# Modulation loads in the units of modulation products, and no such product in the latent stage

## The chip, the cores and the metric

The kernel runs on one core of one Trainium2 chip. The metric is the device time of one execution in microseconds (us). TensorE is PE in the profile (PEld its weight load), VectorE is DVE, ScalarE is ACT, GpSimd is POOL, SyncE is SP. Each engine works through its own instructions strictly in the order in which they were written.

## The reference

Two transformer layers and then a third, modulated one, for 256 tokens of width 2048, all in float32. Cut to what matters here:

```python
x = residual_update(x, mixer_a(rms_norm(x), w_in_a, w_out_a), ..., w_ple_proj[0], w_ple_gate[0])   # 16 stick-breaking heads
kv = shared_kv(x, ..., w_dkv, ..., w_uk, w_uv, cos, sin)                                      # latent k and v, rotary
x = residual_update(x, mixer_b(rms_norm(x), kv, w_in_b, ..., w_uq, w_out_b), ..., w_ple_proj[1], w_ple_gate[1])
# second_block, the modulated layer
mod = silu(c) @ w_ada + b_ada                 # one row of 2048 times 2048 x 12288
sh1, sc1, gt1, sh2, sc2, gt2 = split(mod, 6)
h = rms_norm_2(x) * (1 + sc1) + sh1           # then w_in, a convolution, a sparse attention, gates, w_o
x = x + gt1 * rms_norm_2(mixed)
h = rms_norm_2(x) * (1 + sc2) + sh2           # then a gated feed-forward
x = x + gt2 * rms_norm_2(f)
```

`mod` depends on `c` and `w_ada_2` alone. It can be worked out at any time before the third layer needs it.

## The kernel before

The program is written out by a planner, the class `Run`. The large products stand in a list of blocks, one per 512 columns of a weight matrix (`w_in_a`, `w_out_a`, ..., in the order of the reference). A block is cut into **units**: the six matmuls of 128x512 that multiply two chunks of 128 rows of a weight by one of the two token tiles (`t` = 0 or 1), each chunk as three products of a high and a low part (L421 to L423, or L344 in pairs of blocks), into a PSUM tile `acc` or `sc`. A unit takes some 1.36 us of PE. There are 1695 units, numbered by `self.u`; unit 66 begins at about 87 us of the trace, unit 260 at 397, unit 344 at 523, unit 408 at 616, unit 560 at 869, unit 1016 at 1561, unit 1112 at 1696. Units named below are those numbers.

Every two units need one item of weights: 512 KB loaded by SP into `wst` (4 buffers), then split by ACT into `wh` (L213) and by DVE into the rest `wl` (L214), about ten units ahead (`LEAD`), into 6 buffers each (`RING`). `pump()` writes these out.

After each unit `go`, `pair` or `flipped` calls `side()`. It first continues the small work that hangs behind the blocks (normalisation, attention heads, rotary turns, transposes with `tp` as their PSUM tile), and then the **modulation**. `mod` is worked out on DVE: 24 column chunks `q` of 512 columns by 16 row chunks `k`, 384 products. One product is a load of 256 KB of `w_ada_2` into a tile `ast` (3 buffers, `XBUF`; on POOL's queue, L329) and one DVE instruction that multiplies it by a column of silu(c) and adds it to `ada` (L568 for the first row chunk, L571 for the others). After the sixteenth, `ada_sum` adds `ada` over the partitions: ACT and DVE split it into `adh` (L584) and `adl` (L585), and five units later PE multiplies both by ones (L588, L589), for each half of the chunk.

The list `extra` holds the 384 products with the unit in which each is due. `spread` makes it: it takes the units of two stretches (for chunks 0 to 19 and for 20 to 23) that are `calm`, which leaves out the units around `turns` (12 units before to 19 after a block at which one layer's result is completed or the next one's weights are prepared ahead, or a `w_ple_proj` block) and those around `heads` (from 4 units before the first to 3 after the last of the blocks named there), and spreads the products evenly over the units that are left. `xc` counts products used, `xd` products loaded. A product is used in the first unit that is at or past its due unit; a load may be written up to 12 units ahead of the due unit if one of the three buffers is free. In the kernel before a unit does one of the two, which makes at most one product in two units.

The **latent stage** is `w_dkv` (units 408 to 432), the latent norm, `w_in_b` with POOL, ACT and DVE making the key rope `krr` (L1093) and the latent tiles `ckvh`, `ckvl` (L533, L535), and then `w_uk`, `w_uv`, `w_uq` with the 16 latent heads between them (units 496 to 560): for these heads POOL turns the ropes (L1086 to L1089) out of tiles `nat` that ACT copies from PSUM (L1141), DVE copies keys (`kT`, L1124) and divides (`wide`, L1252, L1254).

Of the kernel before, what the change touches and what calls it, by code (L numbers as in the profile page):

```python
# [29 lines left out]
XBUF = 3  # L30
# [105 lines left out]
class Run:  # L136
# [170 lines left out]
    def side(self):  # L307
        for rec in list(self.urgent):
            if not rec[2] and rec[1] <= self.u:
                self.advance(rec)  # L310
        for rec in self.slow:
            if rec[1] <= self.u:
                self.advance(rec)
        self.urgent, self.slow, self.active = ([r for r in x if not r[2]] for x in (self.urgent, self.slow, self.active))
        if (self.queue and len(self.active) < self.width and self.u >= self.last + self.space
                and all(r[2] for r in self.queue[0][3])):
            rec = self.queue.popleft()
            rec[1] = self.u
            self.active.append(rec)
            self.last = self.u  # L320
        self.step()
        if self.xc < self.xd and self.extra[self.xc][0] <= self.u:
            x = self.extra[self.xc]
            x[2](x[3])
            self.xc += 1
        elif (self.xd < len(self.extra) and self.xd - self.xc < XBUF and self.extra[self.xd][0] - 12 <= self.u):
            x = self.extra[self.xd]
            st = self.main.tile([P, NB], F32, tag="ast", bufs=XBUF, name="ast")
            self.nc.gpsimd.dma_start(st, x[1])  # L329
            x.append(st)  # L330
            self.xd += 1
# [111 lines left out]
def body(ctx, tc, a, out):  # L443
# [117 lines left out]
    def ada_chunk(q, k):  # L561
        c0 = q * NB

        def use(w):
            s = silu_c[:, k : k + 1]
            if k == 0:
                ada_acc[q] = main.tile([P, NB], F32, tag="ada", bufs=2, name="ada")
                nc.vector.tensor_scalar(ada_acc[q], w, s, None, op0=ALU.mult)  # L568
                return
            acc = ada_acc[q]  # L570
            nc.vector.scalar_tensor_tensor(acc, w, s, acc, op0=ALU.mult, op1=ALU.add)  # L571
            if k == 15:
                ada_done.setdefault(q // 4, []).append(run.later(ada_sum(q)))

        return a["w_ada_2"][0, k * P : (k + 1) * P, c0 : c0 + NB], use
# [60 lines left out]
    blocks = []  # L636
# [1226 lines left out]
    def spread(run):  # L1863

        uf = blocks[n_ffn].u0
        calm = lambda lo, hi: [u for u in range(lo, hi) if all(not b - 12 <= u < b + 20 for b in turns)
                               and not heads[0] - 4 <= u < heads[-1] + 4]
        heads = [b.u0 for b in blocks if b.w.tensor.name in (a["w_uk"].tensor.name, a["w_uq"].tensor.name)]
        turns = [b.u0 for b in blocks if b.enter is not None or b.ahead is not None or b.w.tensor.name == a["w_ple_proj"].tensor.name]
        xs = []  # L1870
        uc = conv_block.u0
        for qs, us in ((range(20), calm(100, uc - 30) + calm(uc + 290, uf - 110)), (range(20, 24), calm(uf + 40, uf + 300))):
            todo = [(q, k) for q in qs for k in range(16)]
            for i, (q, k) in enumerate(todo):
                xs.append([us[len(us) * i // len(todo)], *ada_chunk(q, k)])
        return xs

    run = Run(nc, main, psum, blocks, spread)
    run.go()
    ph.close()  # L1880
# [48 lines left out]
```

## Time and profile before

| | |
|---|---|
| median of 3 runs | 2538.36 us (2535.8 to 2538.81) |
| the profiled execution | 2536.7 us, its span 2534.9 us |
| granted TensorE clock, mean over the span | 0.994 |
| PE busy | 2471.3 us, 97% of the span |
| DVE busy | 1814.5 us, 72% |
| ACT busy | 1329.5 us, 52% |
| POOL busy | 283.6 us, 11% |
| moved by DMA | 562.51 MB, mean 222 GB/s |

The busy rows are sums over one execution; they say nothing of a single stage. Where an engine waits, the trace names the instruction that it waited with, the one that released it, the sum, how often and the longest. A DMA issue on POOL's queue counts as an instruction of POOL. The granted clock is the share of the full TensorE clock (2.4 GHz) that the chip gave: 1.00 is the upper level, 0.50 the lower.

### The profile page before, as it was taken

The page shows a single profiled execution, that of the slowest core. Times are in us where ns is not written, and L with a number is a line of the kernel's source. Part 1 is how long each engine was busy: PE and PEld are TensorE (multiplying, and loading weights), DVE is VectorE, ACT ScalarE, POOL GpSimd, SP SyncE. Part 2 cuts the span into 40 slices and gives each one's busy share as a digit, 9 for nine tenths or more (in the row PEclk, how much of TensorE's full clock was granted, in tenths as well). Part 3 has the DMA queues.
Part 4 walks back from the last instruction along what each step waited for, and adds up shares of the span by engine and source line. Part 5 has one row for each costly group of instructions (what it writes and reads, how often), then busy time and mean ns, then how long its engine had stood idle before and what let it go on. Part 6 is the DMA issues. An engine that isn't in the chain of part 4 may idle for free.

```text
span 2534.9 us, 33034 instructions
## 1 busy us (share of the span) xinstructions
PE 2471.3 (97%) x11818; PEld 2051.2 (81%) x11818; DVE 1814.5 (72%) x2492; ACT 1329.5 (52%) x1938; POOL 283.6 (11%) x535
## 2 busy tenths in 40 slices
PE   9999999999899999999999999999999999999998
PEld 7888888878689887878977877888788878888886
DVE  5466677787776667767999867675776787776665
ACT  6555564455555555554544465445644554455453
POOL 2011112112213401000000001100000000000000
PEclk9999999999999999999999999999999999999999
DMA  7577778887786667756656547875577767656563
GB/s 250 172 237 251 253 233 297 283 270 247 264 277 193 195 220 250 230 194 191 188 150 198 176 150 225 286 257 192 176 265 259 238 200 269 223 181 228 184 202 126
DMA packets 272213, 562.51 MB, mean 222 GB/s; under 512 B 20984, under 2 KB 43928, under 8 KB 270000
## 3 DMA queue, kind: packets, MB, share of 16 engines
q1 hardware_dynamic: 236688, 438.56, 53.6%
q0 software_dynamic: 34448, 120.67, 13.9%
q8 instruction: 93, 1.52, 0.2%
q10 hardware_dynamic: 912, 1.17, 0.1%
q14 instruction: 72, 0.59, 0.1%
HBM read 551.86 MB, written 8.45 MB: 221 GB/s over the span
## 4 chain that ended last, share of the span: by engine, by line
PE 85%; DVE 6%; DMA 3%; ACT 2%; issue 2%; POOL 1%; DVEq 0%; POOLq 0%; SPq 0%; ACTq 0%
PE acc L421 17%; PE acc L423 17%; PE acc L422 17%; PE acc L344 7%; PE sc L421 5%; PE sc L423 5%; PE sc L422 5%; PE sc L344 4%; PE pv L344 3%; DVE wl L214 2%; DMA ast<-in_w_ada_dram 2%; PE sc L1205 1%; PE tp L522 1%; ACT wh L213 1%; PE pv L1205 1%
## 5 line engine op out<-in xcount | busy, mean ns | idle before, releaser
L214 DVE TENSOR_TENSOR wl<-wst,wh 128x1024 fp32r<-128x1024 f32 (+2 forms) x758 | 904.3, 1198 | 447.8 <-ACT wh L213 444.6
L213 ACT ACTIVATE wh<-wst 128x1024 fp32r<-128x1024 f32 (+2 forms) x758 | 783.8, 1038 | 728.1 <-PE acc L423 289.2
L421 PE MATMUL acc<-wh,ah 128*128 128x512 f32 (+4 forms) x1630 | 639.8, 393 | 5.6 <-ACT wide L1600 2.9
L422 PE MATMUL acc<-wl,ah 128*128 128x512 f32 (+4 forms) x1630 | 628.0, 385 | 1.5 <-DVE wl L214 1.5
L423 PE MATMUL acc<-wh,al 128*128 128x512 f32 (+4 forms) x1630 | 627.5, 385 | 1.9 <-DVE sst L551 1.9
L329 POOL DMA_DIRECT2D ast<-in_w_ada_dram x384 | 207.7, 541 | 1514.5 <-DVE ada L571 1262.6
L421 PEld LDWEIGHTS acc<-wh,ah 128*128 128x128 f32 x1630 | 308.9, 190 | 64.7 <-ACT wide L1600 3.4
L423 PEld LDWEIGHTS acc<-wh,al 128*128 128x128 f32 x1630 | 308.5, 189 | 62.2 <-DVE al L527 2.1
L422 PEld LDWEIGHTS acc<-wl,ah 128*128 128x128 f32 x1630 | 309.1, 190 | 57.1 <-DVE wl L214 3.3
L571 DVE SCALAR_TENSOR_TENSOR ada<-ast,silu_c,ada 128x512 f32<-128x512 f32 x360 | 268.2, 745 | 61.8 <-DMA ast<-in_w_ada_dram 61.7
L1396 DVE SCALAR_TENSOR_TENSOR cv<-cv,wdw 128x255 f32<-128x255 f32 (+14 forms) x240 | 112.3, 468 | 6.5
L344 PE MATMUL acc<-wh,ah 128*128 128x512 f32 x270 | 105.6, 391 | 0.0
L344 PE MATMUL acc<-wh,al 128*128 128x512 f32 x270 | 105.1, 389 | 0.0
L344 PE MATMUL acc<-wl,ah 128*128 128x512 f32 x270 | 105.1, 389 | 0.0
L421 PE MATMUL sc<-wh,ah 128*128 128x512 f32 x266 | 104.7, 394 | 0.0
L422 PE MATMUL sc<-wl,ah 128*128 128x512 f32 x266 | 103.7, 390 | 0.0
L423 PE MATMUL sc<-wh,al 128*128 128x512 f32 x266 | 103.7, 390 | 0.0
L227 ACT ACTIVATE wh<-wst,cols 128x512 fp32r<-128x512 f32 (+2 forms) x112 | 68.3, 663 | 43.5 <-PE acc L423 27.5
L228 DVE SCALAR_TENSOR_TENSOR wl<-wst,cols,wh 128x512 fp32r<-128x512 f32 (+2 forms) x112 | 72.2, 688 | 13.8 <-ACT wh L227 13.7
L421 PE MATMUL sc<-wh,hh 128*128 128x512 f32 x176 | 68.9, 391 | 0.0
L421 PE MATMUL acc<-wh,hh 128*128 128x512 f32 x176 | 68.8, 391 | 0.0
L423 PE MATMUL acc<-wh,hl 128*128 128x512 f32 x176 | 68.5, 389 | 0.0
(440 smaller groups left out, 3892.1 us busy)
## 6 DMA issues: line engine op xcount, KB each, us to landing
ast<-in_w_ada_dram POOLq DMA_DIRECT2D x384, 256.0 KB, 4.2
wst<-in_w_in_dram SPq DMA_DIRECT2D x144, 512.0 KB
wst<-in_w_in_a_dram SPq DMA_DIRECT2D x120, 512.0 KB
wst<-in_w_down_dram SPq DMA_DIRECT2D x88, 512.0 KB
wst<-in_w_gate_dram SPq DMA_DIRECT2D x70, 512.0 KB
wst<-in_w_up_dram SPq DMA_DIRECT2D x70, 512.0 KB
wst<-in_w_ple_gate_dram SPq DMA_DIRECT2D x64, 512.0 KB
wst<-in_w_in_b_dram SPq DMA_DIRECT2D x40, 512.0 KB
```

The costliest lines, as they stand in the source:

```text
L213: nc.scalar.activation(wh, st, AF.Copy)
L214: nc.vector.tensor_sub(wl, st, wh.bitcast(F32))
L227: nc.scalar.activation(wh[:, c, :], st[:, c, :], AF.Copy, scale=g)
L228: nc.vector.scalar_tensor_tensor(wl[:, c, :], st[:, c, :], g, wh[:, c, :].bitcast(F32), op0=ALU.mult, op1=ALU.subtract)
L329: self.nc.gpsimd.dma_start(st, x[1])
L344: nc.tensor.matmul(banks[x], lhsT=l, rhs=r[:, c, :], start=new and c == k == 0, stop=stop and c == 1 and k == 2, skip_group_check=True)
L421: nc.tensor.matmul(o, lhsT=hi, rhs=wh[:, c, :], start=kc == 0, stop=False)
L422: nc.tensor.matmul(o, lhsT=hi, rhs=wl[:, c, :], start=False, stop=False)
L423: nc.tensor.matmul(o, lhsT=lo, rhs=wh[:, c, :], start=False, stop=kc == b.cp * b.np - 1)
L571: nc.vector.scalar_tensor_tensor(acc, w, s, acc, op0=ALU.mult, op1=ALU.add)
L1205: nc.tensor.matmul(o, lhsT=l, rhs=r, start=start, stop=True, skip_group_check=True)
L1396: nc.vector.scalar_tensor_tensor(acc[:, sft:], u[:, : S - sft], wdw[:, c, k : k + 1], acc[:, sft:], op0=ALU.mult, op1=ALU.add)
```

## The change

Two things are changed. In `side()` the `elif` becomes an `if`: a unit that has used a product may also write a load. In `spread`, `heads` begins at `w_dkv` and no longer at `w_uk`, so that no unit from 404 to 560 is a due unit (before: 492 to 560), and the first stretch begins with unit 66 where it began with 100 (unit 66 stands among the first eight heads of the first layer).

```diff
@@ -323,7 +323,7 @@
             x = self.extra[self.xc]
             x[2](x[3])
             self.xc += 1
-        elif (self.xd < len(self.extra) and self.xd - self.xc < XBUF and self.extra[self.xd][0] - 12 <= self.u):
+        if (self.xd < len(self.extra) and self.xd - self.xc < XBUF and self.extra[self.xd][0] - 12 <= self.u):
             x = self.extra[self.xd]
             st = self.main.tile([P, NB], F32, tag="ast", bufs=XBUF, name="ast")
             self.nc.gpsimd.dma_start(st, x[1])
@@ -1865,11 +1865,11 @@
-        heads = [b.u0 for b in blocks if b.w.tensor.name in (a["w_uk"].tensor.name, a["w_uq"].tensor.name)]
+        heads = [b.u0 for b in blocks if b.w.tensor.name in (a["w_dkv"].tensor.name, a["w_uq"].tensor.name)]
...
-        for qs, us in ((range(20), calm(100, uc - 30) + calm(uc + 290, uf - 110)), (range(20, 24), calm(uf + 40, uf + 300))):
+        for qs, us in ((range(20), calm(66, uc - 30) + calm(uc + 290, uf - 110)), (range(20, 24), calm(uf + 40, uf + 300))):
```

Before, the products are used up to 91 units behind their due units (303 of the 384 late), so that they run on through `turns` and into the latent stage. After, each is used in its due unit. How many products are used in a stretch of units, by the two programs:

| units | what stands there | before | after |
|---|---|---|---|
| 66 to 100 | `w_in_a`, first heads | 0 | 29 |
| 100 to 260 | `w_in_a`, heads | 81 | 137 |
| 260 to 292 | turn to `w_out_a` | 16 | 0 |
| 292 to 324 | `w_out_a` | 16 | 27 |
| 324 to 362 | turn at `w_ple_proj`, `w_ple_gate` | 19 | 0 |
| 362 to 396 | `w_ple_gate` | 17 | 29 |
| 396 to 556 | turn, and the latent stage | 80 | 0 |
| 556 to 596 | after the last latent head | 3 | 3 |
| 596 to 628 | `w_out_b` | 17 | 27 |
| 628 to 662 | turn at `w_ple_proj`, `w_ple_gate` | 8 | 0 |
| 662 to 688 | `w_ple_gate` | 12 | 14 |
| 688 to 1002 | third layer: `w_in_2`, convolution, sparse attention | 1 | 0 |
| 1002 to 1064 | `w_conv_out_2`, `w_attn_out_2`, gates | 32 | 53 |
| 1064 to 1098 | gates | 17 | 1 |
| 1216 to 1480 | feed-forward (chunks 20 to 23) | 64 | 64 |

Within the stretches the pace goes from one product in two units to 0.85 to 0.87 in a unit.

Three places show the order. The first is POOL among the latent heads, at `w_uk` to `w_uq`: `qr` and `rm` are rope tiles of a pair of heads, `nat` the copy that ACT makes, `ast` a modulation tile. Before:

```order
L1086 TENSOR_TENSOR qr_7162<-nat_7160,ropes_69 128x128
L1087 TENSOR_TENSOR rm_7163<-nat_7160,ropes_69 128x2x32
L1088 TENSOR_TENSOR rm_7163<-nat_7160,ropes_69 128x2x32
L1089 TENSOR_TENSOR qr_7162<-qr_7162,rm_7163 128x128
L329 DMA ast_7196<-in_w_ada_2_dram 128x512
L329 DMA ast_7256<-in_w_ada_2_dram 128x512
L329 DMA ast_7302<-in_w_ada_2_dram 128x512
L1086 TENSOR_TENSOR qr_7342<-nat_7340,ropes_69 128x128
```

After, at the same place:

```order
L1086 TENSOR_TENSOR qr_7058<-nat_7056,ropes_69 128x128
L1087 TENSOR_TENSOR rm_7059<-nat_7056,ropes_69 128x2x32
L1088 TENSOR_TENSOR rm_7059<-nat_7056,ropes_69 128x2x32
L1089 TENSOR_TENSOR qr_7058<-qr_7058,rm_7059 128x128
L1086 TENSOR_TENSOR qr_7194<-nat_7192,ropes_69 128x128
```

The loads that stood behind the ropes of one pair of heads and ahead of those of the next are gone from there.

The second is DVE at the end of a block of `w_ple_gate` in the first layer (units 362 to 396): L977 and L978 make the new `x` from a finished block, which PE then transposes. Before:

```order
L214 TENSOR_TENSOR wl_4992<-wst_4905,wh_4991 128x1024
L571 SCALAR_TENSOR_TENSOR ada_4748<-ast_5003,silu_c_80,ada_4748 128x512
L214 TENSOR_TENSOR wl_5013<-wst_4926,wh_5012 128x1024
L977 TENSOR_TENSOR nat_5024<-nat_5024,big_4497 128x512
L978 TENSOR_TENSOR x_3859<-x_3859,nat_5024 128x512
L977 TENSOR_TENSOR nat_5036<-nat_5036,big_4516 128x512
L978 TENSOR_TENSOR x_3861<-x_3861,nat_5036 128x512
L571 SCALAR_TENSOR_TENSOR ada_4748<-ast_5028,silu_c_80,ada_4748 128x512
```

After, at such a block:

```order
L571 SCALAR_TENSOR_TENSOR ada_4635<-ast_5244,silu_c_80,ada_4635 128x512
L571 SCALAR_TENSOR_TENSOR ada_4635<-ast_5265,silu_c_80,ada_4635 128x512
L214 TENSOR_TENSOR wl_5301<-wst_5211,wh_5300 128x1024
L977 TENSOR_TENSOR nat_5312<-nat_5312,big_4806 128x512
L978 TENSOR_TENSOR x_4173<-x_4173,nat_5312 128x512
L571 SCALAR_TENSOR_TENSOR ada_4635<-ast_5274,silu_c_80,ada_4635 128x512
L977 TENSOR_TENSOR nat_5325<-nat_5325,big_4827 128x512
L978 TENSOR_TENSOR x_4175<-x_4175,nat_5325 128x512
L571 SCALAR_TENSOR_TENSOR ada_4635<-ast_5289,silu_c_80,ada_4635 128x512
```

Two products stand in a row ahead of most weight splits, and one stands between the two halves of the new `x`.

The third is DVE in the gates of the third layer (units 1016 to 1064). Before:

```order
L571 SCALAR_TENSOR_TENSOR ada_14103<-ast_14165,silu_c_80,ada_14103 128x512
L214 TENSOR_TENSOR wl_14176<-wst_14053,wh_14175 128x1024
L571 SCALAR_TENSOR_TENSOR ada_14103<-ast_14187,silu_c_80,ada_14103 128x512
L214 TENSOR_TENSOR wl_14201<-wst_14089,wh_14200 128x1024
L585 TENSOR_TENSOR adl_14213<-ada_9430,adh_14212 128x256
L571 SCALAR_TENSOR_TENSOR ada_14103<-ast_14216,silu_c_80,ada_14103 128x512
```

After:

```order
L571 SCALAR_TENSOR_TENSOR ada_14157<-ast_14218,silu_c_80,ada_14157 128x512
L585 TENSOR_TENSOR adl_14274<-ada_9757,adh_14273 128x256
L214 TENSOR_TENSOR wl_14278<-wst_14175,wh_14277 128x1024
L571 SCALAR_TENSOR_TENSOR ada_14157<-ast_14234,silu_c_80,ada_14157 128x512
L571 SCALAR_TENSOR_TENSOR ada_14157<-ast_14244,silu_c_80,ada_14157 128x512
L214 TENSOR_TENSOR wl_14302<-wst_14200,wh_14301 128x1024
L571 SCALAR_TENSOR_TENSOR ada_14157<-ast_14264,silu_c_80,ada_14157 128x512
L571 SCALAR_TENSOR_TENSOR ada_14157<-ast_14290,silu_c_80,ada_14157 128x512
```

One product between two weight splits became two in most gaps.

## Rows read from the trace of the kernel before

**Rows 1.** From the page: busy time of the engines, the chain of work that ended last by engine, the group of the modulation products on DVE, and the DMA issues of modulation tiles (KB of one, median us from issue to landing).

```profile
PE 2471.3 (97%) x11818; PEld 2051.2 (81%) x11818; DVE 1814.5 (72%) x2492; ACT 1329.5 (52%) x1938; POOL 283.6 (11%) x535
...
PE 85%; DVE 6%; DMA 3%; ACT 2%; issue 2%; POOL 1%; DVEq 0%; POOLq 0%; SPq 0%; ACTq 0%
...
L571 DVE SCALAR_TENSOR_TENSOR ada<-ast,silu_c,ada 128x512 f32<-128x512 f32 x360 | 268.2, 745 | 61.8 <-DMA ast<-in_w_ada_dram 61.7
...
ast<-in_w_ada_dram POOLq DMA_DIRECT2D x384, 256.0 KB, 4.2
```

**Rows 2.** The waits of PE in the latent stage (616 to 907 us): the waiting group, the group that released it, us in total, times, longest.

```profile
PE acc L421 <- DVE kT L1124: 3.6, 4, 1.3
PE tp L522 <- DVE ckvl L535: 2.5, 1, 2.5
PE tp L522 <- ACT wh L227: 2.3, 1, 2.3
PE acc L421 <- ACT krr L1093: 2.1, 1, 2.1
PE acc L423 <- DVE sst L551: 1.9, 1, 1.9
PE tp L589 <- DVE adl L585: 1.6, 2, 0.9
...
PE tp L588 <- ACT adh L584: 1.3, 1, 1.3
```

**Rows 3.** The largest wait of DVE, and POOL's wait at its ropes, in the same stage (616 to 870 us).

```profile
DVE ada L571 <- DMA ast<-in_w_ada_dram: 44.0, 16, 5.8
...
POOL qr L1086 <- ACT nat L1141: 56.9, 8, 8.9
```

**Rows 4.** The timeline of POOL, DVE and PE around 811 to 821 us, at one pair of latent heads: start, duration, instruction, and in brackets the idle time before it with its releaser.

```profile
811.52 0.87 POOL L1086 TENSOR_TENSOR qr<-nat,ropes 128x128 f32<-128x128 f32 x1 [8.30 <-ACT nat L1141]
...
814.51 0.58 POOL L329 DMA_DIRECT2D ast<-in_w_ada_dram  x1
...
818.07 0.75 DVE L571 SCALAR_TENSOR_TENSOR ada<-ast,silu_c,ada 128x512 f32<-128x512 f32 x1 [3.94 <-DMA ast<-in_w_ada_dram]
818.74 1.22 DVE L214 TENSOR_TENSOR wl<-wst,wh 128x1024 fp32r<-128x1024 f32 x1
819.87 0.68 DVE L1124 COPY kT<-acc 128x512 f32<-128x512 f32 x1
...
820.61 0.45 PE L421 MATMUL acc<-wh,cqh 128*128 128x384 f32 x1 [1.09 <-DVE kT L1124]
```

**Rows 5.** Stretches of the latent stage and of its first part: start and end, length, busy time of PE, PEld, DVE, ACT and POOL (with instructions), granted clock, DMA share, GB/s; then, from the timeline of PE, the transposes after the wait for `ckvl`.

```profile
616.00:751.00 135.00, 123.11 (x612) 104.25 (x611) 97.33 (x167) 76.04 (x146) 32.96 (x68) 0.96 0.81 266
680.00:685.00 5.00, 2.85 (x8) 1.73 (x6) 2.89 (x7) 1.47 (x6) 1.32 (x3) 0.68 0.58 181
685.00:690.00 5.00, 4.63 (x16) 3.76 (x17) 4.05 (x13) 2.67 (x7) 0.54 (x1) 0.66 0.40 138
...
685.37 0.63 PE L522 MATMUL tp<-ident,nat 128*128 128x128 f32 x4 [2.52 <-DVE ckvl L535]
```

**Rows 6.** The waits of PE at the turns from `w_out_a` (500 to 526 us) and from `w_out_b` (994 to 1019 us), two rows of each, and the first modulation product in the first of them, on DVE's timeline.

```profile
PE tp L522 <- DVE x L943: 2.7, 3, 1.2
PE tp L522 <- PE sc L423: 1.0, 1, 1.0
...
PE tp L522 <- DVE x L943: 2.8, 3, 1.2
PE tp L522 <- issue: 1.7, 1, 1.7
...
501.49 0.75 DVE L571 SCALAR_TENSOR_TENSOR ada<-ast,silu_c,ada 128x512 f32<-128x512 f32 x1 [1.76 <-DMA ast<-in_w_ada_dram]
```

**Rows 7.** One use of a modulation tile on DVE, and the issue of the next load on POOL that waited for it; then the landing times of modulation tiles (issue to landing) in three stretches: 1561 to 1649 us (32 loads), 455 to 480 us (12 loads), 137 to 415 us (87 loads).

```profile
1591.23 0.74 DVE L571 SCALAR_TENSOR_TENSOR ada<-ast,silu_c,ada 128x512 f32<-128x512 f32 x1
...
1592.27 0.54 POOL L329 DMA_DIRECT2D ast<-in_w_ada_dram  x1 [2.78 <-DVE ada L571]
...
DMA to landing us min/median/max: 3.7/4.2/4.8
...
DMA to landing us min/median/max: 4.0/5.4/6.0
...
DMA to landing us min/median/max: 2.9/4.1/6.1
```

**Rows 8.** Stretches with modulation loads, columns as in rows 5: the first heads, the third layer's gates (units 1016 to 1080), and the ten us with the most bytes moved.

```profile
84.00:395.00 311.00, 309.14 (x1495) 258.98 (x1494) 201.52 (x246) 179.21 (x242) 43.03 (x80) 1.00 0.73 232
1561.00:1649.00 88.00, 88.00 (x393) 72.96 (x392) 62.30 (x71) 41.60 (x48) 17.20 (x32) 1.00 0.87 286
432.00:442.00 10.00, 10.00 (x46) 8.29 (x45) 4.71 (x6) 4.16 (x7) 1.08 (x2) 1.00 1.00 406
```

**Rows 9.** Two places where DVE feeds PE, each by its two timelines: at `w_ple_gate` in the first layer (DVE L978, PE L522) and at the end of the first heads (DVE L891, PE L522).

```profile
570.97 0.69 DVE L978 TENSOR_TENSOR x<-x,nat 128x512 f32<-128x512 f32 x1
...
572.35 0.60 PE L522 MATMUL tp<-ident,x 128*128 128x128 f32 x4
...
390.97 0.68 DVE L891 TENSOR_TENSOR wide<-wide,nat 128x512 f32<-128x512 f32 x1
...
392.62 0.60 PE L522 MATMUL tp<-ident,wide 128*128 128x128 f32 x4
```

## The prediction

> **What bounds the kernel now.** I read the page first. PE is busy for 97% of the span, and 85% of the chain that ended last is PE; DVE has 6% of it and DMA 3% [rows 1]. So the time is PE's own work plus the places where PE stands. The change leaves every product and every matmul in place: 384 products before and after, a busy sum that doesn't move. Only PE's waits can change, so next I read PE's waits stage by stage, and then whose work was in front of the releaser.
>
> In the latent stage the reader is to see that most releasers are DVE instructions, and that DVE itself stands there for 44.0 us waiting for modulation tiles, up to 5.8 us at a time [rows 2, 3]. The cause is an order on POOL. POOL waits 8.30 us for the ACT copy `nat` before a rope turn; a modulation load written behind that turn is issued at 814.51; DVE, in order, waits 3.94 us for its tile and reaches the product at 818.07, the weight split at 818.74 and the copy `kT` at 819.87; PE waits 1.09 us for `kT` [rows 4]. A slow copy on ACT thus travels through POOL, a DMA and DVE to PE. After such a wait the granted clock drops for a few us: 0.68 and 0.66 in the two stretches around the `ckvl` wait, against 0.96 over the first 135 us of the stage [rows 5].
>
> At the two turns PE waits for the new `x` (L943) [rows 6]. DVE has more than it can do there, and modulation products stand among its work.
>
> **What the change removes.** A profiled execution of 2536.7 us is the base; it is 1.7 us below the median of the runs shown, so I add 1 us at the end.
>
> Latent stage: 80 products leave units 396 to 556 and no load stands behind a rope (first order piece). Waits that lose their cause: `kT` 3.6, `ckvl` 2.5, `krr` 2.1, `sst` 1.9, `adl` 1.6, `adh` 1.3 [rows 2], together 13.0 us. The last two vanish surely, as no chunk ends there. `kT` and `ckvl` have a product in front of them on DVE. For `krr` and `sst` I infer it from DVE's load, so the low end leaves them out: 9.0. The 2.3 us for `wh` L227 stay, being ACT's own work. The clock: 0.04 of 135 us is 5.4 us lost; the two 5 us stretches lose 1.6 and 1.7, which leaves 2.1 for a third [rows 5]. The first follows the wait that stays; the second follows `ckvl` and the third goes with `krr`. I take 1.7 for each of these two, 3.4. Latent stage: 16.4 us (9 to 17). What is late next there is ACT (wh L227, the copies), which frees nothing more.
>
> Turns: 19 products leave units 324 to 362 and 8 leave 628 to 662. Each takes 0.67 us of a full DVE (818.07 to 818.74 [rows 4]), and the first one of a turn also stood 1.76 us for its tile [rows 6]. The PE waits shown at both turns sum to 2.7 + 1.0 + 2.8 + 1.7 = 8.2 us. Four products and a wait per turn are 4 x 0.67 + 1.76 = 4.4 us, more than the 3.7 and 4.5 that PE stands, nearly, so I take 7 (4 to 8). Sum of the gains: **23.4** (13 to 25).
>
> **What it adds.** The products go into fewer units, at 0.85 to 0.87 per unit where it was 0.5. DVE's work has room: in the first heads it is busy for 201.5 of 311 us [rows 8], and 85 more products at 0.67 are 57. The load issue in the unit of a use costs POOL 0.54 us, and POOL is idle there. What isn't free is the ring of three `ast` buffers. A load can be issued only when a product is done: from the start of a product to the next issue were 1592.27 - 1591.23 = 1.04 us [rows 7]. Then it lands, then the product can start. So three products take 1.1 us plus a landing. The new order puts two products ahead of most weight splits (third piece); if the tile is late, the split `wl`, `adl` or a feed of PE behind it is late.
>
> The landing: median 4.2 us at 286 GB/s in the gates, 5.4 (4.0 to 6.0) at 455 to 480 us, 4.1 in the first heads, the shortest 2.9 [rows 7, 8]. After the change the gates want 524 KB of weights in two units of 1.375 us (88 us for 64 units), 191 GB/s, and 262 KB in some 1.9 us, 136 GB/s: 327 GB/s. That lies above the 286 of the row with 4.2, and more loads share the queues at a time. I take **4.7 us**, between the 4.2 and the 5.4: three products in 5.8 us, 1.93 each. Ends: 4.2 (1.77 each) and 5.4 (2.17).
>
> Without any lag the plan itself would want 41 x 262 KB in 66 us, 163 GB/s, and so 354 GB/s with the weights. The trace has moved more: 406 GB/s over ten us, with all DMA engines busy [rows 8]. The Trainium skill, "DMA: Bandwidth & Descriptors", in "Where 436 GB/s comes from", says of one core's transfers from HBM that a limit of about 358 GB/s binds them, which speaks against this change: by it the plan would run at the limit, with the landings and the 2553 us of the third rival below. That row of 406 GB/s disagrees, so the page adds nothing to that rival's chance.
>
> By stretch, in DVE's lag behind the order's plan:
>
> Gates, units 1016 to 1064: 41 products in 48 x 1.375 = 66 us by plan, 41 x 1.93 = 79 by the ring: 13 us late at the end. A split is written ten units, 13.75 us, ahead of its use; it takes 1.22 itself [rows 4] and about as much on ACT before: 11.4 us of cover. `adl` has five units, 6.9 us. So PE loses 1.6 at a split and a little more at an `ada_sum`: 3 (0 to 10).
>
> `w_ple_gate`, units 362 to 396: 29 products; a unit is 1.45 us there (523 to 616 us for 64 units), so 1.66 per product by plan, 0.27 behind on each. Two feeds of PE stand in it: DVE ends L978 at 571.66 and PE begins at 572.35, 0.7 us of cover [rows 9]. After 13 products DVE is 3.5 us late, 2.8 past the cover; after 14 more another 3.8 us. 7 (2 to 14).
>
> First heads, units 66 to 260: 166 products in some 311 us [rows 8] are 1.87 each, about the ring's pace. Where no attention makes units longer, the plan is 1.66, and DVE falls 4 to 5 us back, then recovers. Feeds have little cover (391.65 to 392.62, 1.0 us [rows 9]). 7 (2 to 14).
>
> Units 292 to 324, 596 to 628 and 662 to 688: the lag is made up in the 12 free units ahead of each turn: 1 (0 to 3). Half-clock stretches after new waits: 2 (0 to 4), one of 1.7 us at least [rows 5]. The feed-forward has the same 64 products in 264 units and no new crowding: 0; were its cover gone, a late tile would cost one landing's excess, 1 us. The last chunk of the first twenty is done at unit 1064 and not 1098; nothing that ends the path waits for it.
>
> Sum of the costs: **20** (4 to 45). Net 23.4 - 20 = 3.4 us faster: 2536.7 - 3.4 + 1 = **2534 us**.
>
> **The rivals.** First, the ring costs little: landings stay at 4.2 us, a product takes 1.77. Then the gates fall only 41 x 1.77 - 66 = 7 us back, inside their cover but for an `adl` (1), `w_ple_gate` is 0.11 x 27 - 0.7 = 2.3 late, the first heads 2, clock 1: cost about 6. 2536.7 - 23.4 + 6 = **2519**. For it: the shortest landings are 2.9 and 3.7, and DMA was at 0.87 in the gates, not full. Against it: the row at 455 to 480 us.
>
> Second, the ring never limits at all: with the shortest landing, 2.9 us, three products take 4.0 us, 1.33 each, under every plan, and the whole gain stays: **2513 or 2514**. The Trainium skill, on the same page in "Anatomy of one DMA — SWDGE (gpsimd) path", gives a transfer 2.0 us and its bytes by 436 GB/s: 2.6 us for 262 KB, an estimate that would make this the case. The medians of 4.1 to 5.4 [rows 7] speak against it, as they hold the company of the weight loads.
>
> Third, slower: landings of 5.0 us or more, since three loads in flight share the queues with the weights. Then a product takes 2.03 us: the gates 17 us late at the end (10 lost), `w_ple_gate` 10, the first heads 166 x (2.03 - 1.87) = 27 us behind, half of it covered by the heads' own waits (14), the rest 6: 40. 2536.7 - 23.4 + 40 = **2553**. It decides from 4.8 us on, where costs equal gains. For it: 5.4 between 455 and 480.
>
> Fourth, only half of the gain comes, since ACT's copies and POOL's ropes (56.9 us of POOL's waiting [rows 3]) are late by themselves and PE waits for them directly: 2536.7 - 11.7 + 20 = **2545**. That the change doesn't do what it says is ruled out by the order of the rows (first piece).
>
> **How the numbers follow.** Forecast 0.35, first rival 0.30, second 0.05, third 0.20, fourth 0.10. A difference counts from 0.2%, 5 us, which is about what a measurement of this kernel can tell from none. Forecast: 0.10 faster, 0.20 within, 0.05 slower; first: 0.28 and 0.02; second: 0.05 faster; third: 0.20 slower; fourth: 0.03 within, 0.07 slower. Faster 0.43, same 0.25, slower 0.32. The range from 2515 to 2555 leaves out the second rival and the worse half of the third. The likeliest case alone would be 2528 to 2541.
>
> **What would show it.** In the latent stage the waits for `kT`, `ckvl`, `adl` and `adh` should be gone, DVE's 44.0 us for tiles too, and the granted clock of 616 to 751 us should rise from 0.96 to 0.98 or more. At the turns the L943 waits should go under 1 us each. In the gates and at `w_ple_gate` DVE should wait for `ast` and PE for `wl`, `adl` and L978; the landing there decides: 4.2 the first rival, 4.7 mine, 5.0 the third. I am wrong if PE still waits for `kT` (fourth), or if DVE waits for no tile in the gates (second).

## The result, and the profile after

The changed kernel takes 2553.66 us (median of 4 runs, 2552.79 to 2558.86), the kernel before 2537.14 us beside it: a ratio of 1.0069, 95% interval 1.0057 to 1.0081. It is slower by 16.5 us. The forecast was 2534 us, 3 us faster; the time lies inside the stated range, at its upper end, where the third rival stood. Why it came there is another matter, below.

The profiled execution spans 2551.1 us, the one before 2534.9. To see where 16.2 us came from, I matched the matmuls of both programs unit by unit and took the start of each unit. How much longer each stretch of units took after the change:

| units | what stands there | forecast, us | measured, us |
|---|---|---|---|
| 66 to 272 | first heads | +7 | +26.2 |
| 324 to 362 | turn | -3.5 | -2.6 |
| 362 to 396 | `w_ple_gate` | +7 | +9.7 |
| 408 to 564 | latent stage | -16.4 | -25.5 |
| 640 to 652 | turn | -3.5 | -2.3 |
| 1016 to 1080 | gates | +3 | +7.9 |
| the rest | | +3 | +2.8 |
| sum | | -3.4 | +16.2 |

Every stretch moved the way that was forecast. The gains were 30 us instead of 23, the costs 47 instead of 20, and 26 of them lie in the first heads.

The page of the changed kernel: PE's and DVE's busy time, and the modulation loads with the median time from issue to landing.

```profile
PE 2480.9 (97%) x11818; PEld 2057.2 (81%) x11818; DVE 1816.3 (71%) x2492; ACT 1326.2 (52%) x1938; POOL 288.3 (11%) x535
...
ast<-in_w_ada_dram POOLq DMA_DIRECT2D x384, 256.0 KB, 4.0
```

PE is busy for 9.6 us more with the same matmuls [rows 1]: that is clock, whose mean over the span fell from 0.994 to 0.990, and 0.004 of 2481 us is 9.9. The loads landed no later than before.

The waits of PE in the latent stage after the change, 616 to 907 us (waiting group, releaser, us in total, times, longest):

```profile
PE tp L522 <- DVE x L978: 3.0, 1, 3.0
PE pv L1205 <- DVE wide L1252: 1.6, 2, 0.8
PE tp L522 <- ACT wh L227: 1.5, 1, 1.5
PE tp L1151 <- POOL qr L1089: 0.5, 1, 0.5
PE tp L522 <- DVE ckvl L535: 0.4, 1, 0.4
```

The first row still belongs to `w_ple_gate`. `kT`, `krr`, `sst`, `adl` and `adh` are gone, `ckvl` fell from 2.5 to 0.4, `wh` from 2.3 to 1.5 [rows 2]. At the first turn no wait for L943 is left, and at the second, from 1000 to 1040 us, two short ones, where each turn had 2.7 or 2.8 [rows 6]:

```profile
PE tp L522 <- DVE x L943: 0.8, 2, 0.5
```

The first heads, where PE waited 1.9 us in two waits before and DVE for no tile: PE's waits from 84 to 440 us, and below them DVE's waits from 84 to 415 us.

```profile
PE tp L522 <- DVE wide L891: 7.2, 3, 4.8
PE sc L850 <- ACT sph L846: 5.6, 4, 2.3
PE pv L834 <- ACT e L855: 2.3, 1, 2.3
```

```profile
DVE ada L571 <- DMA ast<-in_w_ada_dram: 43.2, 41, 2.9
...
DVE ada L568 <- PE tp L604: 8.4, 2, 5.9
...
DVE ada L568 <- DMA ast<-in_w_ada_dram: 3.7, 3, 1.9
```

PE stands for 15.1 us. DVE stands 47 us for modulation tiles in 44 waits, none over 2.9 us, and twice for something that the prediction doesn't know: the first product of a column chunk (L568) waits for a transpose on PE (L604). How that reaches PE is seen on the timeline of DVE, with PE's two rows around it:

```profile
384.75 0.49 DVE L568 TENSOR_SCALAR ada<-ast,silu_c 128x512 f32<-128x512 f32 x1 [5.90 <-PE tp L604]
...
390.25 0.68 DVE L891 TENSOR_TENSOR wide<-wide,nat 128x512 f32<-128x512 f32 x1
...
384.48 0.23 PE L604 MATMUL tp<-ident,ada 16*128 16x16 f32 x1
391.08 1.09 PE L522 MATMUL tp<-ident,wide 128*128 128x128 f32 x4 [4.77 <-DVE wide L891]
```

The accumulator `ada` has two buffers. Of every fourth chunk it is held longer, since the finished row of `mod` is loaded back into it as columns (L601) and transposed (L604). In the order before, a chunk took 32 units and nobody noticed. Now a chunk takes 19, the chunk after the next wants the buffer before L604 has run, and behind the L568 that waits there stand three more products, two splits `wl` and an `adl` ahead of L891, for which PE waits 4.77 us.

The stretches after the change (start and end, length, busy time of PE, PEld, DVE, ACT and POOL, granted clock, DMA share, GB/s): the first heads, the first part of the latent stage, `w_ple_gate`.

```profile
84.00:440.00 356.00, 340.28 (x1602) 282.34 (x1601) 269.61 (x353) 193.35 (x275) 91.23 (x167) 0.98 0.84 279
649.00:770.00 121.00, 119.18 (x630) 103.30 (x629) 68.78 (x119) 74.15 (x137) 9.40 (x22) 1.00 0.65 204
571.00:633.00 62.00, 56.37 (x244) 46.26 (x243) 52.07 (x67) 29.35 (x46) 13.93 (x26) 0.92 0.80 263
```

The first heads had a clock of 1.00 and have 0.98: 7 us of 356 are lost to the lower level of the clock, half as much again as PE waits there. `w_ple_gate`, with two waits for L978 that sum to 5.6 us, has 0.92: another 5 us. The latent stage rose from 0.96 to 1.00 [rows 5].

PE's waits in `w_ple_gate` (571 to 640 us) and in the gates (1555 to 1720 us), where the kernel before had none:

```profile
PE tp L522 <- DVE x L978: 5.6, 2, 3.0
```

```profile
PE tp L589 <- DVE adl L585: 4.4, 3, 2.4
```

And the landing of modulation tiles after the change, at 84 to 415 and at 1565 to 1645 us:

```profile
DMA to landing us min/median/max: 2.8/3.9/5.9
...
DMA to landing us min/median/max: 2.9/3.8/6.2
```

Before, the medians there were 4.1 and 4.2 [rows 7]. So the third rival's time came, and its mechanism (landings of 5.0 us) didn't.

### The profile page after: what moved, and what is told of

Its sections match the earlier page's. It is cut to its first block, busy times and chain, and to the rows that moved or that the text cites. A ratio compares the mean times of both kernels' runs of the same rounds, so it can differ in the third digit from the quotient of the medians.

```text
span 2551.1 us, 33063 instructions
## 1 busy us (share of the span) xinstructions
PE 2480.9 (97%) x11818; PEld 2057.2 (81%) x11818; DVE 1816.3 (71%) x2492; ACT 1326.2 (52%) x1938; POOL 288.3 (11%) x535
## 5 line engine op out<-in xcount | busy, mean ns | idle before, releaser
L571 DVE SCALAR_TENSOR_TENSOR ada<-ast,silu_c,ada 128x512 f32<-128x512 f32 x360 | 269.5, 749 | 102.4 <-DMA ast<-in_w_ada_dram 100.3
```

## The experiments

Theories: **A**, the ring of three `ast` tiles: it turns in 1.04 + 3.9 + 0.1 us, 1.7 us for a product, and the plan wants one in 1.66 where no attention stretches the units; each landing above the median puts DVE behind, the plan leaves no slack to catch up, and the feeds of PE have under 1 us of cover [rows 9]. **B**, not the tiles but DVE's own time: two products in a row ahead of a feed. **C**, the two accumulators. The third rival, slow landings, had fallen with the rows above.

**Half of the loads.** Odd products multiply the tile of the even one before, so that three tiles serve six products. DVE's instructions are the same.

```diff
...
+            if self.xd % 2 == 0:
+                self.shared = self.main.tile([P, NB], F32, tag="ast", bufs=XBUF, name="ast")
+                self.nc.gpsimd.dma_start(self.shared, x[1])
+            x.append(self.shared)
```

> The changed kernel, but every odd modulation product multiplies the tile of the even one before it, so that half of the 384 loads are left out (the modulation values change) and three tiles serve six products. Every instruction of DVE stays where it is. Theory A (the ring of three tiles puts DVE behind): DVE's waits for tiles (100.3 us on L571 in the changed kernel) fall under 10, the first heads lose 8 to 10 us instead of 26 (what the accumulators still cost), w_ple_gate about 3 instead of 9.7, the gates about 1 instead of 8: 2553.7 - 16 - 7 - 7 = 2524 us, ratio to before about 0.995. Theory B (two products in a row ahead of a feed, DVE's own time): the same feeds are late with every tile in time, at least 2545 us, ratio above 1.003. Theory C (the two accumulators): 2545 to 2550, PE's 4.8 us wait for L891 stays.

Measured: 2516.25 us, ratio 0.9919 (0.9904 to 0.9934). DVE waits for no tile any more. `w_ple_gate` takes 0.3 us less than in the kernel before (it had cost 9.7), the gates 1.1 more (7.9), the first heads 16.4 more (26.2), where I had expected 8 to 10. B is out: with every product where it was, `w_ple_gate` loses nothing, and the gates no more than the PE time of four pairs of `ada_sum` that moved into them (1.3 us by the price of a pair below). What stays in the heads is C, for the most part. DVE's waits there:

```profile
DVE ada L570 <- PE tp L606: 14.2, 2, 8.1
```

L570 and L606 are L568 and L604 in this kernel. With the tiles in time DVE comes to the accumulator earlier and stands there longer, 14.2 us instead of 8.4.

**The accumulator free earlier.** The load of the row back (L601) is left out, a constant is transposed.

```diff
-        m = acc[:16, 0:P]
-        nc.scalar.dma_start(m, mod_rows[i])
+        m = ident[:16, 0:P]
```

> The changed kernel, but the load of a modulation row back as columns (L601) is left out and a constant is transposed in its place, so that the accumulator of every fourth column chunk is free about nine units earlier (the modulation values change). Theory C (the first product of a chunk stands 2.5 and 5.9 us on DVE for the accumulator of the chunk before the last, and L891 behind it): L568 waits for no L604, PE's 4.8 us for L891 and 2.2 to 2.3 of another wait go, with 2 to 5 us of half clock: 2542 to 2547 us, ratio 1.002 to 1.004. Theory A (tiles): DVE stands for tiles instead, 2549 to 2554 us, ratio 1.005 to 1.007.

Measured: 2546.75 us, ratio 1.0039 (1.0026 to 1.0052). The waits for L604 are gone, the first heads lose 21.2 us instead of 26.2, `w_ple_gate` still 10.2 and the gates 7.1. C is real and the smaller part.

**Both edits.**

> Both of the edits before: half of the loads left out, and a constant in place of the row that is loaded back. Theories A and C together: first heads lose 0 to 3 us, 2512 to 2518 us, ratio 0.990 to 0.993. Theory B: at least 2540 us, ratio above 1.001.

Measured: 2505.96 us, ratio 0.9876 (0.9859 to 0.9892), better than I expected. The first heads lose 5.5 us, the gates 1.1, `w_ple_gate` nothing. So A and C together are 20.7 of the 26.2 us in the heads; A alone gave back 9.8 and C alone 5.0, since whichever is left hides part of the other. What the 5.5 are is partly seen on PE's timeline of the changed kernel, where an `ada_sum` stands between two units:

```profile
197.13 0.38 PE L588 MATMUL tp<-adh,ones_r 128*128 128x256 f32 x1
197.35 0.28 PE L589 MATMUL tp<-adl,ones_r 128*128 128x256 f32 x1
197.46 0.40 PE L421 MATMUL acc<-wh,ah 128*128 128x512 f32 x1
```

A pair takes 0.33 us of PE and a chunk has two. Units 66 to 272 hold 20 pairs where they held 10: 3.3 us, which left the latent stage in exchange. In the run with both edits PE's waits in the heads sum to 3.1 us where the kernel before had 1.9, and its granted clock of 0.98 from 350 to 420 us is some 1.4 us more.

**The due list alone**, with the old `elif`:

```diff
-        if (self.xd < len(self.extra) and ...
+        elif (self.xd < len(self.extra) and ...
```

> The new due list of the change with the old elif: a unit uses or loads. 98 products stand in units 66 to 260 (before 81, after 166), 19 and 10 at the turns, 56 in units 396 to 564 (before 83, after 3). Theory A and C: at one product in two units neither ring is short, so nothing is lost in the first heads, and the latent stage keeps its waits in units 408 to 456 (16 of its 25 us): 2531 to 2537 us, ratio 0.998 to 1.000. If the early start or the crossing of heads itself were the cost: 2545 us or more.

Measured: 2534.11 us, ratio 0.9988 (0.9978 to 0.9997). The heads cost 1.0 us. Of the latent stage units 496 to 564 lose their waits (7.8 us less) and units 408 to 456 keep them (1.9 more), `krr` even with 4.6:

```profile
PE acc L421 <- ACT krr L1093: 4.6, 1, 4.6
PE tp L522 <- ACT wh L227: 2.2, 1, 2.2
PE tp L522 <- DVE ckvl L535: 2.0, 1, 2.0
PE acc L423 <- DVE sst L551: 1.9, 1, 1.9
```

So the list without the `if` empties the latent heads but not `w_dkv`, as the products are late. The early start is no cost in itself.

**A fourth tile in the heads.** The first run left out bytes as well as waits for tiles. Here all 384 loads are made; up to unit 240 one more tile stands in the ring, and the row loaded back has its own tile there.

```diff
+        early = self.u < 240
+        if (self.xd < len(self.extra) and self.xd - self.xc < XBUF + early and ...
+            if early and self.xd % 4 == 3:
+                st = self.fourth()
...
-        m = acc[:16, 0:P]
+        m = ph.tile([16, P], tag="adm") if i < 2 else acc[:16, 0:P]
```

> The changed kernel with all of its loads and bytes, but up to unit 240 a fourth modulation tile stands in the ring, and the row that is loaded back (L601) has a tile of its own there, so that the accumulator is free earlier. Nothing else is changed, w_ple_gate and the gates keep three tiles. Theory A with C (ring of three, two accumulators): the first heads lose 3 to 7 us instead of 26: 2553.7 - 20 = 2534 us (2530 to 2538), ratio 0.997 to 1.001. If it was the bytes and not the number of tiles (half of the loads were left out in the run before): only the accumulators' part comes back, 2543 to 2548 us, ratio 1.003 to 1.005.

Measured: 2533.22 us, ratio 0.9990 (0.9980 to 0.9999). The number of tiles it is, not the bytes: with every load made, the heads get 14.8 us back, where an accumulator free earlier had given back 5.0 alone. DVE's waits for tiles in the heads, and the landing there:

```profile
DVE ada L575 <- DMA ast<-in_w_ada_dram: 10.5, 16, 1.8
...
DMA to landing us min/median/max: 2.9/4.4/6.7
```

L575 is L571 here. Landings are longer in this run (4.4 after 3.9), and still DVE's waits fall from 43.2 to 10.5. The heads lose 11.4 us where I expected 3 to 7; `w_ple_gate` (+11.0) and the gates (+7.6), which kept three tiles, lose what they lost.

**A slower pace, in four runs.** The same `if` and the same three tiles; only the stretches are longer.

```diff
-        for qs, us in ((range(20), calm(66, uc - 30) + calm(uc + 290, uf - 110)), ...
+        for qs, us in ((range(20), calm(66, uc - 30) + calm(uc + 290, uf - 76)), ...
```

> The changed kernel with the second stretch of due units ended 34 units later (at unit 1098), which gives 0.78 products in a unit of the first heads instead of 0.86 (152 instead of 166 of them there). Theory A: a ring of three turns once in 1.04 + 4.0 + 0.1 us, 1.71 us for a product, against a plan of 1.82 now (1.66 in the changed kernel): DVE makes up for a late tile, the first heads lose 6 to 12 us instead of 26, w_ple_gate 2 to 4 instead of 9.7, the gates 1 to 4 instead of 8: 2521 to 2534 us, ratio 0.994 to 0.999. If the loss goes with the number of products in a stretch (a price for each), a tenth less: 2548 to 2550 us, ratio above 1.004.

For 0.67 and for the two runs behind it, part of the latent stage is opened again as well (36 is 56 and 66 in the later ones, and 76 is 90 in the last):

```diff
-                               and not heads[0] - 4 <= u < heads[-1] + 4]
+                               and not heads[0] - 4 <= u < heads[0] + 48 and not heads[-1] - 36 <= u < heads[-1] + 4]
```

> As the run with 0.78, and units 456 to 520 of the latent stage take products again (43 of them), while units 404 to 456 and 520 to 560 stay free: 0.67 products in a unit, 2.1 us for each in the first heads. Theory A: three tiles are enough nearly everywhere, the first heads lose 0 to 3 us, w_ple_gate and the gates 0 to 2 each; the latent stage keeps 20 of its 25 us, since units 456 to 520 hold no wait in the changed kernel's gain but 1 us: 2511 to 2518 us, ratio 0.990 to 0.993. If products among the latent heads cost by themselves, 2522 us or more.

> As the run with 0.67 products in a unit, but the products in the latent stage end at unit 500 and not at 520 (31 instead of 43 of them), which makes 0.70 in a unit. Theory A with the price of products among the latent heads (8.6 us were lost in units 496 to 520 of the run before, behind a 5.1 us wait of PE for POOL's ropes): that loss goes, the first heads pay 0 to 2 us more: 2517.5 - 8 + 1 = 2510 us (2506 to 2514), ratio to before 0.988 to 0.991. If that wait has nothing to do with the products beside the heads: 2517 us or more, ratio above 0.992.

> As the run before, the latent stage's products ending at unit 490 (25 of them) and the second stretch at unit 1084: 0.72 products in a unit, 1.96 us for each in the first heads where the ring turns in 1.7. Theory A: the first heads lose 2 to 5 us (at 0.67: 1, at 0.78: 9), w_ple_gate 1 to 3, the gates 0 to 2: 2510 to 2518 us, ratio 0.990 to 0.993.

Measured, with DVE's waits for tiles (L571) at 84 to 415 us and the us that stretches lose against the kernel before:

| products in a unit | us, ratio (interval) | DVE's wait, times | first heads | `w_ple_gate` | gates |
|---|---|---|---|---|---|
| 0.86, the change | 2553.66, 1.0069 (1.0057 to 1.0081) | 43.2, 41 | 26.2 | 9.7 | 7.9 |
| 0.78 | 2530.51, 0.9977 (0.9967 to 0.9988) | 28.6, 29 | 9.5 | 7.1 | 1.3 |
| 0.72, latent to 490 | 2513.32, 0.9911 (0.9898 to 0.9924) | 15.3, 19 | 3.0 | 2.1 | 0.5 |
| 0.70, latent to 500 | 2514.44, 0.9916 (0.9904 to 0.9928) | 5.7, 13 | 2.9 | 0.1 | 0.7 |
| 0.67, latent to 520 | 2517.45, 0.9928 (0.9910 to 0.9945) | 3.2, 8 | 2.0 | 0.7 | 0.7 |

A tenth fewer products take away two thirds of the loss in the heads. This is what a ring does whose turn is about as long as the plan's step, and not what a price for each product would do. Both rings gain by a slower pace, so these runs don't tell A from C: in the heads DVE's waits for L604 fall as well, from 8.4 us to 5.9 at 0.78, 1.9 at 0.72, 0.7 at 0.70 and none at 0.67. Two things were missed. At 0.78, `w_ple_gate` still lost 7.1 where I expected 2 to 4, and units 1080 to 1098, which now hold products up to the next turn, lost 9.5:

```profile
PE acc L421 <- DVE cv L1628: 6.0, 2, 4.9
```

In the run with 0.67, units 496 to 520 lost 8.6 us behind one wait of PE for POOL's rope, and the latent stage kept 16 us where I expected 20; the run whose products end at unit 500 lost 1.3 in those units. PE's wait in either, at 740 to 800 us:

```profile
PE tp L1151 <- POOL qr L1089: 5.1, 1, 5.1
```

```profile
PE tp L1151 <- POOL qr L1089: 0.5, 1, 0.5
```

The way is on the timelines of DVE, POOL and PE in the run with 0.67:

```profile
748.87 0.49 DVE L568 TENSOR_SCALAR ada<-ast,silu_c 128x512 f32<-128x512 f32 x1 [4.92 <-DMA gate<-ada]
749.65 0.55 POOL L329 DMA_DIRECT2D ast<-in_w_ada_dram  x1 [6.03 <-DVE ada L568]
751.74 0.93 POOL L1086 TENSOR_TENSOR qr<-nat,ropes 128x128 f32<-128x128 f32 x1
755.62 0.47 PE L1151 MATMUL tp<-ident,qr 128*128 128x128 f32 x1 [5.13 <-POOL qr L1089]
```

It is C again. The accumulator of the twelfth chunk is held longer still, since a row `gate` is stored out of it (L617). The first product of the chunk after the next waits 4.92 us for it, the load on POOL waits for that product's tile, and the rope stands behind the load. In the run that ends at unit 500, DVE waits as long for the accumulator (4.91 us, up to 733.03 us), but POOL has no rope to turn until 750.22, and PE waits 0.5 us. So the cost among the latent heads is that of the accumulator, where a load stands ahead of a rope, and not of the products by themselves. The run at 0.70 came out at 2514.44, just above my 2506 to 2514. The runs at 0.70 and 0.72 can't be told apart; both beat the kernel before by some 0.85% and the changed one by 1.5%.

## Why the prediction failed

**What held.** The latent chain over POOL, a tile and DVE to PE was right: the named waits went, and so the fourth rival fell. The turns gave 4.9 us (forecast 7). Units before a turn did make up their lag. The kinds of cost, and that they lie in the ring, were right too; the runs with half of the loads and with the fourth tile show it.

**Mis-sized, to the better.** The latent stage gave 25.5 us, not 16.4. The waits of PE for kT, ckvl, krr, sst, adl, adh and partly `wh` that went sum to 13.4 us; the clock gave back its whole 5.4 and not 3.4; and five chunks of `ada_sum`, 0.66 us of PE each, moved out, 3.3 us that I hadn't counted and that came back as a cost in the heads. About 3 us are not traced.

**The step that failed** is the term "First heads ... 7 (2 to 14)", measured 26.2. I had compared the ring's pace with an average over the stretch (1.87 us for a product) and let lag be recovered. Three things were wrong in it. First, where units are short the plan wants 1.66, the ring gives 1.7 at the median and landings scatter from 2.8 to 5.9: there is nothing to recover with, and DVE waits 44 times. Second, the accumulators weren't looked at, although the change nearly halves a chunk's time: a tile with two buffers that is held for 24 units after its chunk's end was safe at 32 units a chunk and isn't at 19. Third, the clock: I allowed 2 us in all for the stretches at the lower level. The rows show 7 in the first heads and 5 in `w_ple_gate` alone. The runs give the sizes: tiles in time take 9.8 of the 26.2 us away, an accumulator free earlier 5.0, both 20.7.

**The landing** of 4.7 us was wrong as well, and in the other direction. Had I worked with the 3.9 measured, the model would have given the first rival's 2519 or a little less. So the right size of loss in the third rival was reached by a wrong price, and it is luck that the time lies inside the stated range: the ring was the bound at ordinary landings already. The second rival, that the ring never limits, fell: DVE stood 47 us for tiles in the first heads, where it had stood for none before. The Trainium skill, "DMA: Bandwidth & Descriptors", in "Anatomy of one DMA — SWDGE (gpsimd) path", puts a transfer at 2.0 us plus its bytes at 436 GB/s; an estimate from that is 2.6 us for a load of 256 KB. The measured median of 3.9 us beside the weight loads disagrees with it.

**Gates and `w_ple_gate`.** 7.9 for a forecast of 3 and 9.7 for 7: inside their bounds. In the gates PE waited for `adl` 4.4 us in three waits and for no `wl`; the rest of the loss is clock (0.98 from 1570 to 1670 us) and the moved `ada_sum`. `wl` had its ten units of cover, as worked out.

## What to carry to other kernels

When a change packs side work denser, work out the turn of every ring that it passes through (tiles loaded, accumulators, what is held for a tail), and compare it with the shortest step of the plan, not with the average over a stretch. A ring whose turn equals that step loses out of all proportion: here a pace lower by a tenth to a fifth gave back 17 to 24 of 26 us. Count a wait of a few us on TensorE for more than its length where the granted clock falls after it: here 7 us beside 15.1 us of waits, and 5 beside 5.6.

## What the runs showed of the hardware

Loads of 256 KB didn't land later in a denser stretch: median 4.1 us at 232 GB/s before and 3.9 at 279 after in the first heads, with three buffers in either. The median was 4.4 in the run with a fourth tile, and 4.2 with three at the pace of 0.67, so that the fourth load isn't shown to be the cause. In the first heads 15.1 us of waits on PE came with 7 us lost to the lower level of the clock, and in `w_ple_gate` 5.6 us of waits with 5.
